# First layer's first channel product: 12 of 16 slabs as seven products of half sums, hidden chunks of 512

## The chip, the cores and the metric

The kernel runs on one core of a Trainium2 chip. The metric is the time of the program on the device, in microseconds (us), as the median of repeated runs. An engine executes its instructions in order: TensorE (PE: matmuls; its weight loads are listed as PEld), VectorE (DVE), ScalarE (ACT), GpSimd (POOL) and SyncE (SP, which issues nearly all transfers). Between engines, semaphores hold an instruction back until what it reads is written, or what it overwrites has been read.

## What is computed

Two layers over 768 tokens, 512 latent and 256 context, each of width 1024. A layer has a token-mixing sub-layer (convolution and attention) and a channel sub-layer, an MLP with squared ReLU. Shift, scale and gate of each sub-layer come from a modulation vector through `w_ada`.

```python
def sqrelu_mlp(h, w1, w2):
    return jnp.square(jax.nn.relu(h @ w1)) @ w2
...
        x = x + gx2 * sqrelu_mlp(modulate(rmsnorm(x, norm2_g[i]), sx2, ax2), w_mlp1[i], w_mlp2[i])
        if not last:
            h_ctx = h_ctx + gc2 * sqrelu_mlp(modulate(rmsnorm(h_ctx, norm2_g[i]), sc2, ac2),
                                             w_mlp1[i], w_mlp2[i])
```

`w_mlp1` is 1024 x 4096, `w_mlp2` 4096 x 1024. The change concerns `h @ w1` of the first layer, where all 768 tokens go through; in the last layer only the 512 latent tokens do.

## The kernel before

Each fp32 operand is split into a part of less precision and its residue, "hi" and "lo" (`split`, lines 76 and 77: the hi on ACT, the lo on DVE or POOL), and each product is three matmuls, hi x hi, hi x lo, lo x hi (`mm3`, lines 109 to 111). Tokens are the columns of a matmul; the features lie on the 128 partitions, in 8 pieces `k`.

The first layer's channel sub-layer begins when the norm `norm_mod` (line 341 scales on DVE, 345 shifts on ACT, 349 takes residues on DVE, others on POOL; `nsq`, `acc`, `nc`, `ms`, `dg`, `nb` are the squares, their sum and its root) writes `h2hh` and `h2hl`, the hi and lo of the modulated tokens, in three token groups: columns 0, 256 and 512 (the last is the context). The residual stream is `X`. Then four chunks of 1024 hidden features follow, loop `for cch in range(4)` from line 1436. In a chunk four slabs of 256 columns of `w_mlp1` are loaded (`r_w`, split into `h_w` and `l_w`), and `hidden` makes 128 hidden features of a token group as 8 x 3 matmuls into a PSUM bank `f`, then Relu, Square and Square on ACT (1443 to 1445, with the scratch `fr`) and the residue on DVE (1446): `fh` and `fl`. A group that starts at column 0 uses two banks of one pool, the groups that start at 256 or 512 two of another. In the first chunk the first two slabs go by three groups of 256 tokens, since the norm delivers so; all other slabs by 512 and 256. Then `out_slabs` multiplies the chunk's hidden values by 1024 rows of `w_mlp2` (banks `r`) and adds the gated result to `X` (line 1360).

Beside it runs the modulation product of the next layer, in steps between blocks (`ada_step`, `ada_rows`): 48 loads `ar` of 512 KB of `w_ada`, each multiplied by the two vectors and summed into `adaac` on DVE (line 282), then transposed and reduced (`adat`, `adp`). The next layer's small parameters are loaded ahead of it (`layer_params`: `sm`, `lp`, `cs`).

The source code gives order and priorities; a scheduler puts each engine's instructions into a row, and pools of a fixed number of buffers decide what can be issued when. Line 1420 opens the pool of the modulation's loads; the scratch tiles `fr` have three buffers of their own, the norm's scratch `nu` three others.

## Time and profile before

| | us |
|---|---|
| median of 3 runs (lowest, highest) | 2323.01 (2318.35, 2323.18) |
| the profiled execution | 2321.48 |
| its span | 2319.7 |
| first matmul of the first layer's hidden blocks | 820.94 |
| stage shown below | 820 to 1364 |

The profile is one execution. PE, DVE and so on are engines; an entry names line, engine, operation, and the tiles written and read, with partitions x elements and a count. A list of groups has the busy time and the mean length of one in ns, then the idle time of the engine ahead of them with what ended it. In a timeline a row has its start and its length. A row of stretches has the busy time of each engine, then the granted clock of PE, the share of the transfer engines that is busy, and GB/s.

### The profile page before, as it was taken

The numbers are of one execution on the slowest core, as the hardware profiler recorded it, in microseconds if no ns is written. First come the engines' busy times: TensorE is split into PE (matmuls) and PEld (weight loads), VectorE is DVE, ScalarE is ACT, GpSimd is POOL, SyncE is SP. The second block draws the span as 40 slices with busy tenths as digits, with TensorE's granted clock in tenths as the row PEclk, the third lists the DMA queues.
The fourth block names the chain that finished last, engine by engine and source line by source line (L and its number), as shares of the span: only waits on it lengthen the run. The fifth ranks groups of instructions, "written<-read, shape, count | busy, mean of one in ns | idle before, by whom it ended". The sixth has DMA issues, their size and how long they took to land.

```text
span 2319.7 us, 36413 instructions
## 1 busy us (share of the span) xinstructions
PE 2254.4 (97%) x14554; PEld 2022.3 (87%) x14554; DVE 1551.9 (67%) x2720; ACT 1027.0 (44%) x1997; POOL 684.4 (30%) x789
## 2 busy tenths in 40 slices
PE   8999999999999999999999998999999999999999
PEld 6999998888878998888888998999977879888887
DVE  6777776599657445555545567776759965757673
ACT  5555655522323263242524345565643333654542
POOL 1966764110000042323232347676611000100000
PEclk9999999999999999999999999999999999999999
DMA  9211111134534323433434422111113423442251
GB/s 309 63 37 41 46 47 45 44 132 141 161 128 155 106 66 118 128 108 124 131 102 135 110 65 58 44 37 49 44 62 123 134 86 115 155 127 91 73 182 37
DMA packets 217770, 229.48 MB, mean 99 GB/s; under 512 B 7472, under 2 KB 197376, under 8 KB 217472
## 3 DMA queue, kind: packets, MB, share of 16 engines
q1 hardware_dynamic: 217600, 227.15, 30.7%
q8 instruction: 114, 1.87, 0.3%
q14 instruction: 56, 0.46, 0.1%
HBM read 211.36 MB, written 15.77 MB: 98 GB/s over the span
## 4 chain that ended last, share of the span: by engine, by line
PE 81%; DVE 9%; POOL 4%; ACT 3%; DMA 2%; issue 1%; SPq 0%; DVEq 0%; POOLq 0%; ACTq 0%
PE f L109 6%; PE f L110 6%; PE f L111 6%; PE r L109 6%; PE r L111 6%; PE r L110 6%; PE gt L109 2%; PE qk L109 2%; PE gt L110 2%; PE gt L111 2%; PE qk L110 2%; PE qk L111 2%; DVE cacc L1163 2%; PE o L109 2%; PE o L110 2%; PE o L111 2%
## 5 line engine op out<-in xcount | busy, mean ns | idle before, releaser
L109 PE MATMUL f<-h2hh,h_w 128*128 128x512 f32 (+1 forms) x832 | 282.1, 342 | 1.7 <-ACT h2hh L76 1.5
L110 PE MATMUL f<-h2hl,h_w 128*128 128x512 f32 (+1 forms) x832 | 282.7, 341 | 1.0 <-POOL h2hl L77 1.0
L111 PE MATMUL f<-h2hh,l_w 128*128 128x512 f32 (+1 forms) x832 | 281.5, 340 | 0.0
L77 POOL TENSOR_TENSOR l_w<-r_w,h_w 128x1024 fp32r<-128x1024 f32 x64 | 158.5, 2498 | 334.9 <-ACT h_w L76 334.9
L1163 DVE SCALAR_TENSOR_TENSOR cacc<-z,cols,cacc 128x783 f32<-128x783 f32 (+1 forms) x240 | 207.7, 916 | 0.3
L109 PE MATMUL qk<-h_wqk,h1h 128*128 128x256 f32 x640 | 182.6, 288 | 2.1 <-ACT rw L755 1.3
L109 PE MATMUL r<-fh,h_w 128*128 128x256 f32 (+1 forms) x576 | 183.6, 319 | 0.0
L110 PE MATMUL r<-fl,h_w 128*128 128x256 f32 (+1 forms) x576 | 183.4, 319 | 0.0
L111 PE MATMUL r<-fh,l_w 128*128 128x256 f32 (+1 forms) x576 | 183.2, 318 | 0.0
L110 PE MATMUL qk<-l_wqk,h1h 128*128 128x256 f32 x640 | 180.2, 284 | 0.0
L111 PE MATMUL qk<-h_wqk,h1l 128*128 128x256 f32 x640 | 176.3, 284 | 0.3 <-POOL h1l L77 0.3
L110 PEld LDWEIGHTS f<-h2hl,h_w 128*128 128x128 f32 x832 | 157.5, 190 | 19.4 <-POOL h2hl L77 1.8
L109 PEld LDWEIGHTS f<-h2hh,h_w 128*128 128x128 f32 x832 | 156.6, 189 | 20.5 <-ACT h2hh L76 1.9
L927 DVE TENSOR_REDUCE st<-S 128x1 f32<-128x768 f32 (+1 forms) x160 | 134.4, 845 | 57.7 <-PE S L925 56.5
L111 PEld LDWEIGHTS f<-h2hh,l_w 128*128 128x128 f32 x832 | 157.3, 189 | 17.4
L282 DVE SCALAR_TENSOR_TENSOR adaac<-ar,cvec,adaac 128x256 f32<-128x256 f32 x336 | 144.2, 493 | 20.5 <-ACT adaac L279 15.2
L930 ACT ACTIVATE e<-S,st 128x768 f32<-128x768 f32 (+1 forms) x160 | 131.0, 821 | 40.1 <-DVE st L927 39.8
L76 ACT ACTIVATE h_w<-r_w 128x1024 fp32r<-128x1024 f32 x96 | 96.4, 1051 | 101.2 <-issue 44.5
L109 PE MATMUL gt<-h1h,h_wg 128*128 128x512 f32 (+1 forms) x384 | 138.2, 360 | 0.0
L110 PE MATMUL gt<-h1l,h_wg 128*128 128x512 f32 (+1 forms) x384 | 136.7, 356 | 0.0
L111 PE MATMUL gt<-h1h,l_wg 128*128 128x512 f32 (+1 forms) x384 | 136.5, 356 | 0.0
L109 PEld LDWEIGHTS qk<-h_wqk,h1h 128*128 128x128 f32 x640 | 122.1, 191 | 4.4 <-ACT rw L755 1.5
(307 smaller groups left out, 6636.3 us busy)
## 6 DMA issues: line engine op xcount, KB each, us to landing
r_w<-in_w_mlp_dram SPq DMA_DIRECT2D x64, 1024.0 KB, 5.3
ada<-in_w_ada_dram SPq DMA_DIRECT2D x24, 1024.0 KB, 5.6
ar<-in_w_ada_dram SPq DMA_DIRECT2D x48, 512.0 KB, 3.5
r_wqk<-in_w_in_dram SPq DMA_DIRECT2D x32, 512.0 KB, 5.1
r_wg<-in_w_in_dram SPq DMA_DIRECT2D x16, 1024.0 KB, 5.1
r_wv<-in_w_in_dram SPq DMA_DIRECT2D x8, 1024.0 KB, 5.2
r_wao<-in_w_attn_out_dram SPq DMA_DIRECT2D x8, 1024.0 KB, 5.2
r_wo<-in_w_out_dram SPq DMA_DIRECT2D x8, 1024.0 KB, 5.3
```

What stands on the lines that cost most here:

```text
L76: nc.scalar.activation(out=hi, in_=src, func=AF.Copy)
L77: return (lo_eng or nc.vector).tensor_tensor(out=lo, in0=src, in1=f32(hi), op=ALU.subtract)
L109: nc.tensor.matmul(ps, sh, mh, start=first, stop=False)
L110: nc.tensor.matmul(ps, sh, ml, start=False, stop=False)
L111: nc.tensor.matmul(ps, sl, mh, start=False, stop=last)
L282: nc.vector.scalar_tensor_tensor(out=a[:, q], in0=r[:, j], scalar=cvec[:, k, q : q + 1], in1=a[:, q], op0=ALU.mult, op1=ALU.add)
L927: nc.vector.tensor_reduce(out=st[:, m : m + 1], in_=S[:, :nkey], axis=AX.X, op=ALU.max, negate=True)
L930: nc.scalar.activation(out=e[:, :nkey], in_=S[:, :nkey], func=AF.Exp, bias=st[:, m : m + 1], accum_out=st[:, 2 + m : 3 + m])
L1163: nc.vector.scalar_tensor_tensor(out=ca[cc][:, :CV], in0=zt[cc][:, t : t + CV], scalar=wcol, in1=ca[cc][:, :CV], op0=ALU.mult, op1=ALU.add)
```

## The change

The hidden features go in eight chunks of 512 (two slabs of 256). Chunks 0 and 7 are made as before, by `hidden`. In chunks 1 to 6 each slab is seen as a 2 x 2 block product (features in halves of 512, hidden columns in halves of 128, tokens in halves of 384), and `seven` makes it from seven products instead of eight: sums and differences of weight quarters (`sums_f`, `sums_b`, on DVE) by sums and differences of token quarters (`token_sums`, on DVE, kept as hi and lo in `TS`, one in place of a quarter that is saved to DRAM and brought back before chunk 7). A product (`product`) is 4 pieces x 3 matmuls of 384 columns into one of the four banks of `mi_`; the sums of products go to `G` on DVE, Relu and squares on ACT to `F`, a single buffer for the hidden values. `second` multiplies each of chunks 0 to 5 by 512 rows of `w_mlp2`; the last two go together through `out_slabs`. The raw weights are in pieces of half a slab with three buffers.

The scratch of the small parameters, of the modulation sums and of the first chunk's `fr` now comes from the norm's three buffers (tag "u"). The modulation loads are 96 x 256 KB, with two buffers; the first eight slabs of 256 columns are multiplied by both vectors, the other sixteen, two at a time, by the latent one alone. Modulation steps start with the first hidden block.

```diff
+    def t2k(name):
+        if state["nt"]:
+            return state["tp"].tile([P, 512], F32, tag="t2k", bufs=state["nt"], name=name)
+        return state["xp"].tile([P, 512], F32, tag="u", bufs=3, name=name)
...
+        if state["nraw"] == 3:
+            rs = [state["tp"].tile([P, half, shape[1]], F32, tag="raw", name=f"r_{name}_{n}", bufs=3)
+                  for n in range(2)]
...
+        plan = [(s, 2 * k, 2) for s in range(8) for k in range(4)]
+        plan += [(s, k, 1) for s in range(8, 24, 2) for k in range(8)]
...
+            r = state["tp"].tile([P, 512], F32, tag="araw", bufs=2, name=f"ar{i}_{s}_{k}")
+            r = r.rearrange("p (k n) -> p k n", k=nq)
+            nc.sync.dma_start(r, rows(w_ada[i], 256 * s, 512 // nq)[:, k : k + nq])
...
+            state["tp"], state["nraw"], state["nt"] = gp, 3, 0
+            HT, HK = NT // 2, KT // 2
+            N0, N1, K0, K1 = slice(0, HT), slice(HT, NT), slice(0, HK), slice(HK, KT)
+            tt = nc.vector.tensor_tensor
+            F = gp.tile([P, 2, HK, NT], F32R, tag="F", name="F")
+            TS = gp.tile([P, 3, 2, HK, HT], F32R, tag="TS", name="TS")
+            TF = TS.rearrange("p a b k n -> p (a b k n)")
+            G = gp.tile([P, 4, HT], F32, tag="G", name="G")
+            GF = G.rearrange("p a n -> p (a n)")
+            F7 = TF[:, : 2 * HK * NT].rearrange("p (b k n) -> p b k n", b=2, k=HK)
+            b12_d = dpool.tile([2, P, HK, HT], F32, name="b12_d")
+            hl2 = h2h, h2l
+            B11, B12, B21, B22 = ([t[:, k, n] for t in hl2]
+                                  for k, n in ((K0, N0), (K0, N1), (K1, N0), (K1, N1)))
+            T1, T3, T4 = ([TS[:, a, j] for j in range(2)] for a in range(3))
+            T2 = B12
...
+            def squares(x, hi, lo):
+                nc.scalar.activation(out=hi, in_=x, func=AF.Square)
+                nc.scalar.activation(out=x, in_=x, func=AF.Square)
+                state["done"] = tt(out=lo, in0=x, in1=f32(hi), op=ALU.subtract).ins
...
+            def token_sums():
+                for j in range(2):
+                    nc.sync.dma_start(b12_d[j], f32(B12[j]))
...
+                g0, g1 = G[:, 0:2], G[:, 2:4]
+                for ks in (slice(0, 2), slice(2, 4)):
+                    b11, b12, b21, b22, t1, t3, t4 = (
+                        [x[:, ks] for x in b] for b in (B11, B12, B21, B22, T1, T3, T4))
+                    yield from sums(g0, f32(b12[0]), (less, b11[0]), (plus, b12[1]), (less, b11[1]))
+                    yield from sums(g1, f32(b22[0]), (less, b12[0]), (plus, b22[1]), (less, b12[1]))
+                    split(*t1, g0)
+                    yield
+                    yield from sums(g0, g1, (plus, b11[0]), (plus, b11[1]))
+                    split(*t3, g1)
+                    yield
+                    yield from sums(g1, g0, (less, b21[0]), (less, b21[1]))
+                    split(*b12, g0)
+                    yield
+                    split(*t4, g1)
+                    yield
+
+            raws, wts, sms = {}, {}, {}
...
+            def sums_f(c, s):
+                sm = sms[c, s] = gp.tile([P, HK, P], F32, tag="sm", name=f"sm{c}_{s}")
+                a11, a12, a21, a22 = quarters(c, s)
+                tt(out=a21, in0=a11, in1=a21, op=ALU.subtract)
+                tt(out=sm, in0=a22, in1=a21, op=ALU.subtract)
+
+            def fill_a(c, s):
+                sm = sms[c, s]
+                a11, a12, s3, _ = quarters(c, s)
+                w = wts["a", c, s] = pair_tiles((4, HK, P), f"a{c}_{s}")
+                for n, src in enumerate((a11, sm, a12, s3)):
+                    split(w[0][:, n], w[1][:, n], src, nc.gpsimd if n == 2 else None)
...
+            def product(w, n, b, name):
+                ps = mi_.tile([P, 512], F32, tag="mi", name=name)[:, :HT]
+                for k in range(HK):
+                    mm3(ps, (w[0][:, n, k], w[1][:, n, k]), (b[0][:, k], b[1][:, k]),
+                        k == 0, k == HK - 1)
+                return ps
...
+                w = wts.pop(("a", c, s))
+                nc.scalar.activation(out=s11, in_=product(w, 0, B11, nm + "1"), func=AF.Copy)
+                tt(out=s22, in0=s11, in1=product(w, 1, T2, nm + "6"), op=ALU.add)
+                fill_b(c, s)
+                if (c, s) == (6, 1):
+                    for j in range(2):
+                        for k in (slice(0, 2), slice(2, 4)):
+                            r = raw_half(f"b12_{j}_{k.start}", (2, HT))
+                            nc.sync.dma_start(r, b12_d[j][:, k])
+                            nc.scalar.activation(out=B12[j][:, k], in_=r, func=AF.Copy)
+                tt(out=s11, in0=s11, in1=product(w, 2, B21, nm + "2"), op=ALU.add)
+                done(0)
+                tt(out=s21, in0=s22, in1=product(w, 3, T3, nm + "7"), op=ALU.add)
+                ahead()
+                w = wts.pop(("b", c, s))
+                ps = product(w, 0, T1, nm + "5")
+                tt(out=s12, in0=s22, in1=ps, op=ALU.add)
+                tt(out=s22, in0=s21, in1=ps, op=ALU.add)
+                done(3)
+                tt(out=s12, in0=s12, in1=product(w, 1, B22, nm + "3"), op=ALU.add)
+                done(1)
+                later()
+                tt(out=s21, in0=s21, in1=product(w, 2, T4, nm + "4"), op=ALU.subtract)
+                done(2)
...
+            for g in halves:
+                for s in range(2):
+                    for m in range(2):
+                        hidden(0, s, m, g, F, xp.tile([P, 512], F32, tag="u", bufs=3,
+                                                      name=f"fr{s}_{m}_{g.start}"))
+                        ada_step()
+                        if (s, m) == (0, 1) and g is CTXS:
...
+            for c in range(7):
+                if c:
+                    seven(c, 0, lambda: next_f(c), lambda: sums_b(c, 1))
+                    seven(c, 1, lambda: next_r(c))
+                if c == 6:
+                    break
+                fill_r(c, 1, (nc.gpsimd, nc.gpsimd))
+                load_f(c + 1, 0)
+
+                def tick(m, g):
+                    if c == 0:
+                        sum_step(2)
+                    else:
+                        ada_step()
+
+                second(c, 0, tick)
+                load_f(c + 1, 1)
+                sums_f(c + 1, 0)
+                fill_a(c + 1, 0)
+                second(c, 1, tick)
+                sums_b(c + 1, 0)
+                drain(sums)
...
+                        o = 512 * ((4 * s + 2 * m + (g is not LAT)) % 3)
+                        hidden(7, s, m, g, F7, GF[:, o : o + 512])
+                        ada_step()
+                        if g is LAT:
+                            ada_step()
```

What the change does to the rows of three engines, at the start of the stage. Names: `nu_n2_0_512` is the norm's scratch for the context group, `f` and `fr` the hidden blocks and their scratch, `adaac` the modulation sums.

On ACT, where the first Relu of a hidden block stands (before: behind the scale of the second group's norm):

```order
L317 ACTIVATE dg_n2_0_256_9121<-cst_75,ms_n2_0_256_9118 128x128 [waits Pool_49]
L1443 ACTIVATE fr0_0_0_0_9424<-f0_0_0_0_9399 128x256 [waits PE_49]
L1444 ACTIVATE fh0_0_0_9383<-fr0_0_0_0_9424 128x256 [waits Activation_49]
L1445 ACTIVATE fr0_0_0_0_9424<-fr0_0_0_0_9424 128x256 [waits Activation_49]
L345 ACTIVATE h2hh0_8460<-nu_n2_0_256_0_9126,ad0_143 128x256 [waits DVE_49]
```

In the changed kernel the same Relu, now line 1481, comes after the last piece of the context group's norm:

```order
L365 ACTIVATE h2hh0_8463<-nu_n2_0_512_6_9335,ad0_143 128x256 [waits DVE_49]
L76 ACTIVATE TS_9350<-G_9351 128x768 [waits DVE_49,PE_49]
L365 ACTIVATE nu_n2_0_512_7_9339<-nu_n2_0_512_7_9339,ad0_143 128x256 [waits DVE_49]
L76 ACTIVATE h2hh0_8463<-nu_n2_0_512_7_9339 128x256 [waits Activation_49]
L1481 ACTIVATE fr0_0_0_9389<-f0_0_0_0_0_9390 128x256 [waits DMAHW0_49,PE_49,Pool_49]
L1473 ACTIVATE F_9349<-fr0_0_0_9389 128x256 [waits Activation_49]
```

It has moved past 29 rows: the norm of two groups, four squares and one split of a token sum. On PE before, the third block of the first group follows directly on the second:

```order
L110 MATMUL f0_0_1_0_9429<-h2hl0_8461,h_w1_0_0_0_9222 128x256
L111 MATMUL f0_0_1_0_9429<-h2hh0_8460,l_w1_0_0_0_9223 128x256
L109 MATMUL f0_0_2_0_9459<-h2hh0_8460,h_w1_0_0_1_9288 128x256 [waits Activation_49]
L110 MATMUL f0_0_2_0_9459<-h2hl0_8461,h_w1_0_0_1_9288 128x256
L111 MATMUL f0_0_2_0_9459<-h2hh0_8460,l_w1_0_0_1_9289 128x256
```

Now two blocks of the second group come in between, and then the third block (`f0_0_1_0_0`) stands behind the context group's norm and the small parameters:

```order
L125 MATMUL f0_0_0_1_256_9580<-h2hh0_8463,l_w1_0_0_0_9226 128x256
L354 MATMUL nc_n2_0_512_9297<-cst_75,acc0_2_8454 128x1 [waits DVE_49,PE_49]
L343 MATMUL nb_n2_0_512_9306<-dg_n2_0_512_9303,cst_75 128x256 [waits DVE_49]
L182 MATMUL smps1_9355<-cst_75,sm1_9353 128x128 [waits DMAHW0_49,PE_49]
L182 MATMUL smps1_9355<-cst_75,sm1_9353 128x128
L123 MATMUL f0_0_1_0_0_9467<-h2hh0_8463,h_w1_0_0_1_9291 128x256 [waits Activation_49]
```

Between the second and the third block of the first group stand the 48 matmuls of two blocks of the second group and these five small ones, and the third block waits for ACT. On DVE before, the residues of the first chunk's context group and the first modulation sums:

```order
L1446 TENSOR_TENSOR fl0_0_2_9388<-fr0_0_2_512_9724,fh0_0_2_9387 128x256 [waits Activation_49]
L1446 TENSOR_TENSOR fl0_0_3_9390<-fr0_0_3_512_9754,fh0_0_3_9389 128x256 [waits Activation_49]
L1446 TENSOR_TENSOR fl0_0_4_9392<-fr0_0_4_0_9792,fh0_0_4_9391 128x512 [waits Activation_49]
L282 SCALAR_TENSOR_TENSOR adaac1_0_9799<-ar1_0_9797,cvec_332,adaac1_0_9799 128x256 [waits DMAHW2_49]
L282 SCALAR_TENSOR_TENSOR adaac1_0_9799<-ar1_0_9797,cvec_332,adaac1_0_9799 128x256 [waits DVE_49] x4
```

In the changed kernel, ahead of the eighth block: the residues `F` of the second group, token sums into `G` and modulation sums in turn, and a split of `G` that ACT begins (line 76) and DVE ends (line 77).

```order
L1475 TENSOR_TENSOR F_9349<-fr1_1_0_9502,F_9349 128x256 [waits Activation_49]
L301 SCALAR_TENSOR_TENSOR adaac1_0_9423<-ar1_0_4_9428,cvec_332,adaac1_0_9423 128x256 [waits DVE_49]
L77 TENSOR_TENSOR TS_9350<-G_9351,TS_9350 128x768 [waits Activation_49]
L301 SCALAR_TENSOR_TENSOR adaac1_0_9423<-ar1_0_4_9428,cvec_332,adaac1_0_9423 128x256 [waits DVE_49] x2
L1475 TENSOR_TENSOR F_9349<-fr0_0_256_9538,F_9349 128x256 [waits Activation_49]
L1490 TENSOR_TENSOR G_9351<-h2hh0_8463 128x768 [waits DVE_49]
L301 SCALAR_TENSOR_TENSOR adaac1_0_9423<-ar1_0_6_9464,cvec_332,adaac1_0_9423 128x256 [waits DMAHW5_49,DVE_49]
L1490 TENSOR_TENSOR G_9351<-G_9351,h2hl0_8464 128x768 [waits DVE_49]
```

Token sums and modulation sums have moved in among the residues; before, the modulation began only after the residues of the context group.

More of the change, by code (lines that the diff above doesn't have):

```diff
@@ L1408, in mlp1_slab @@
         def mlp1_slab(cch, s):
-            w1[cch, s] = load_slab(rows(w_mlp1[i], 1024 * cch + 256 * s, 256),
+            w1[cch, s] = load_slab(rows(w_mlp1[i], (1024 if last else 512) * cch + 256 * s, 256),
                                    f"w1_{i}_{cch}_{s}", lo_eng=None if last else nc.gpsimd)
@@ L1491, in after @@
             def after(s):
-                if fin:
-                    nc.sync.dma_start(xs_d[i + 1][:, 2 * s : 2 * s + 2, :],
-                                      X[:, 2 * s : 2 * s + 2, :])
+                nc.sync.dma_start(xs_d[i + 1][:, 2 * s : 2 * s + 2, :],
+                                  X[:, 2 * s : 2 * s + 2, :])
             out_slabs(
                 lambda s: load_slab(
-                    w_mlp2[i][1024 * cch : 1024 * cch + 1024, 256 * s : 256 * s + 256]
-                    .rearrange("(k p) n -> p k n", p=P), f"w2_{i}_{cch}_{s}", lo_eng=nc.gpsimd),
-                lambda k: (fh[k], fl[k]), gate2, f"r{i}_{cch}",
-                norm1 if fin else None, after, tick=ada_step, ahead=
-                (lambda: first.update(w=qk_slab(i + 1, 0, nc.gpsimd)),
-                 v_first) if fin else ())
-        if not last:
-            rpool.__exit__(None, None, None)
+                    w_mlp2[i][3072:4096, 256 * s : 256 * s + 256]
+                    .rearrange("(k p) n -> p k n", p=P), f"w2_{i}_{s}", lo_eng=nc.gpsimd),
+                lambda k: tuple((F if k < HK else F7)[:, j, k % HK] for j in range(2)),
+                gate2, f"r{i}", norm1, after, ahead=
+                (lambda: first.update(w=qk_slab(i + 1, 0, nc.gpsimd)), v_first))
             state["ada_done"] = True
-            ada_gain(Ln, 1)
+            ada_gain(Ln, 1, ns=1)
             L = Ln
```

234 lines of the change are left out of this document (154 added, 80 removed).

## The prediction

> **What bounds the kernel now.** The busy table of the page comes first, then the chain that ended last, then the busy time by stretches of the first layer's channel sub-layer.
>
> ```profile
> PE 2254.4 (97%) x14554; PEld 2022.3 (87%) x14554; DVE 1551.9 (67%) x2720; ACT 1027.0 (44%) x1997; POOL 684.4 (30%) x789
> PE 81%; DVE 9%; POOL 4%; ACT 3%; DMA 2%; issue 1%; SPq 0%; DVEq 0%; POOLq 0%; ACTq 0%
> 820.00:1364.00 544.00, 542.97 (x3415) 491.80 (x3413) 285.87 (x598) 204.89 (x376) 170.70 (x80) 1.00 0.36 112
> 820.00:860.00 40.00, 38.97 (x311) 37.65 (x310) 20.11 (x47) 26.51 (x67) 18.44 (x15) 1.00 0.17 54
> 1985.00:2310.00 325.00, 325.00 (x1516) 272.32 (x1516) 208.04 (x273) 154.75 (x213) 2.98 (x4) 1.00 0.33 109
> ```
>
> PE carries 81% of the chain. The stage that is changed runs from 820 to 1364 us; in a row of stretches the columns are PE, PEld, DVE, ACT, POOL, clock, DMA share, GB/s. PE is busy for 542.97 of 544.00 us, at clock 1.00. DVE has 286 us of work there, ACT 205, POOL 171. So the stage is as long as its matmuls, and fewer columns through PE shorten it as long as nobody else becomes late. The last row is the last layer's channel sub-layer, which already uses seven products (of 512 columns): 325.00 of 325.00 us busy, so the scheme as such can be fed.
>
> **What is removed: PE time.** A matmul costs the distance between starts, not its length, since they overlap.
>
> ```profile
> 899.74 0.39 PE L109 MATMUL r<-fh,h_w 128*128 128x512 f32 x1
> 900.42 0.39 PE L109 MATMUL r<-fh,h_w 128*128 128x512 f32 x1
> ...
> 827.07 0.28 PE L111 MATMUL f<-h2hh,l_w 128*128 128x256 f32 x1
> 829.95 0.28 PE L111 MATMUL f<-h2hh,l_w 128*128 128x256 f32 x1
> ```
>
> Three of 512 columns take 0.68 us, 0.2267 each; 24 of 256 take 2.88 us, 0.120 each. For 384 columns the middle, 0.173 (estimate; its bounds are those two). A slab of 256 hidden columns cost 2 blocks x 8 k x 3 = 48 matmuls of each width: 48 x 0.3467 = 16.64 us. As seven products it costs 7 x 4 x 3 = 84 of 384: 14.56 us. Twelve slabs save 12 x 2.08 = **25.0 us**. The four plain slabs and the second product keep their matmuls and widths. With PE dense, the profiled execution's 2321.5 us would become 2296.5.
>
> **What is added: DVE time, most of it at the start.** New on DVE are twenty wide ops of token sums and their residues, the weight sums, the sums of products, and the modulation product of the next layer, which starts earlier. In the order of the changed kernel, DVE goes from the third norm op of the second column group (after 827 us) to the last residue but one of the first chunk's hidden values, through 56 two-operand ops of 256 (22 of the norm, 34 of the modulation), 15 differences of 256, 18 ops of 768, one of 1024, two transposes and two reductions of 512, and some 15 small ones. The prices:
>
> ```profile
> 826.39 1.27 DVE L341 SCALAR_TENSOR_TENSOR nu_n<-X,A,nb_n 128x256 f32<-128x256 f32 x3 [5.06 <-PE nb_n L323]
> 827.57 0.42 DVE L1446 TENSOR_TENSOR fl<-fr,fh 128x256 fp32r<-128x256 f32 x1
> ...
> 875.79 0.42 DVE L1446 TENSOR_TENSOR fl<-fr,fh 128x256 fp32r<-128x256 f32 x1
> 876.13 2.06 DVE L282 SCALAR_TENSOR_TENSOR adaac<-ar,cvec,adaac 128x256 f32<-128x256 f32 x5
> ...
> L77 DVE TENSOR_TENSOR l_w<-r_w,h_w 128x1024 fp32r<-128x1024 f32 x32 | 38.0, 1221 | 30.8 <-ACT h_w L76 30.7
> L77 DVE TENSOR_TENSOR h2hl<-fr,h2hh 128x512 fp32r<-128x512 f32 x16 | 11.0, 685 | 1.4 <-ACT h2hh L76 1.4
> L292 DVE STREAM_TRANSPOSE adat<-adaac 128x512 f32<-128x512 f32 x24 | 16.9, 703 | 0.0
> L293 DVE TENSOR_REDUCE adp<-adat 128x16 f32<-128x512 f32 x24 | 16.5, 688 | 0.8
> ```
>
> Three norm ops fill 826.39 to 827.57: 0.39 each. A difference of 256 fills 875.79 to 876.13: 0.34. An op of 768 isn't in this stage; its bounds are 0.685 and 1.221, the middle is 0.95, less 0.08 for overlap as in the rows above: 0.87. The sum: 56 x 0.39 + 15 x 0.34 + 18 x 0.87 + 1.14 + 2 x 1.35 + about 3 = **49 us**, against 34.6 us of PE (288 matmuls of 256) in the same place. In the kernel before DVE had 20.11 us in those first 40 us.
>
> That this delays PE follows from the orders. The scratch of the first hidden blocks is now one of the three buffers that the norm uses. So on ACT the first Relu stands behind the whole norm of the context group, and PE, whose banks for that group are full after four blocks, has nothing but the small matmuls of that norm in between. The norm's time in the kernel before:
>
> ```profile
> 835.08 0.98 DVE L361 TENSOR_TENSOR acc<-acc,nsq_so 128x256 f32<-128x256 f32 x2 [0.50 <-ACT nsq_so L360]
> 839.25 0.16 DVE L312 TENSOR_SCALAR ms_n<-nc_n 128x2 f32<-128x2 f32 x1 [2.84 <-PE nc_n L334]
> 839.55 0.70 POOL L313 TENSOR_TENSOR ms_n<-ms_n,mhalf 128x2 f32<-128x2 f32 x1 [4.29 <-DVE ms_n L312]
> 840.29 0.48 DVE L319 TENSOR_SCALAR dg_n<-cst,ms_n 128x128 f32<-128x128 f32 x2 [0.88 <-POOL ms_n L313]
> ```
>
> The last squares were summed at 836.1; the chain through POOL to the scale takes 840.8 - 839.2 = 1.6 us and two small matmuls, so the norm ops start between 836 and 838.5 (ACT has twelve ops less ahead, which may win two us). Four blocks end near 834: PE waits from there. DVE then does eight norm ops, four residues and five of the sums of 768 in order, 9 us, so the first Relu comes near 848. From there on each Relu stands behind a split of the token sums on ACT, which waits for DVE: the Relu that releases the eighth block stands behind the split that waits for the 16th wide op. Up to that op DVE has 26 x 0.39 + 16 x 0.87 + 5 x 0.34 + 3 = 28.8 us from 836 to 838.5, and perhaps 1.5 of waits for POOL's residues: 866 to 869. PE would have come to that block at 820.9 + 168 x 0.12 = 841. Five blocks are left, 14.4 us: the second product begins at about 882 to 885 instead of 820.9 + 34.6 = 855.5, that is 27 us late. The kernel before lost some 3 us here (1.03 us idle in its first 40, the rest in stretched matmuls). **Net 24 us**, bounds 16 (below, the lighter start) and 31 (the wide ops at 1.15, 18 x 0.28 more, and 2 us of holds).
>
> PE also comes back slowly from an idle stretch:
>
> ```profile
> 1742.52 0.60 PE L109 MATMUL cg<-h1h,h_wcg 128*128 128x512 f32 x1 [2.49 <-ACT sg L704]
> 1742.92 0.63 PE L110 MATMUL cg<-h1l,h_wcg 128*128 128x512 f32 x1
> 1743.34 0.63 PE L111 MATMUL cg<-h1h,l_wcg 128*128 128x512 f32 x1
> ...
> 1746.28 0.39 PE L109 MATMUL cg<-h1h,h_wcg 128*128 128x512 f32 x1
> 1746.50 0.40 PE L110 MATMUL cg<-h1l,h_wcg 128*128 128x512 f32 x1
> ```
>
> After 2.49 us idle the matmuls start 0.42 apart until 1746, then 0.22: eight times 0.2, 1.6 us lost. DVE sets when the waits above end, so only the last of them can cost this on top (ahead of the five blocks): it lies within the 27. [...]
>
> **Later chunks.** In the second product of chunk 1 and the products of chunk 2, DVE has 56 modulation ops (22 us), 16 residual adds, 22 ops of 384 on products, 20 of 512 on weights, one of 1024 and four transposes with reductions, by
>
> ```profile
> L1360 DVE SCALAR_TENSOR_TENSOR X<-r,ad,X 128x256 f32<-128x256 f32 x47 | 22.5, 480 | 21.2 <-PE r L111 20.9
> L1360 DVE SCALAR_TENSOR_TENSOR X<-r,ad,X 128x512 f32<-128x512 f32 x24 | 18.0, 751 | 68.4 <-PE r L111 68.4
> ```
>
> less 0.08 each (0.40 and 0.67; 384 between them, 0.47 as the ops do without the scalar): 22 + 8.6 + 10.3 + 12.2 + 1.1 + 5.4 = 60 us, while PE needs 33.3 + 29.1 = 62.4. A share of 96% leaves no room for holds:
>
> ```profile
> 854.76 4.97 POOL L77 TENSOR_TENSOR l_w<-r_w,h_w 128x1024 fp32r<-128x1024 f32 x2 [2.59 <-ACT h_w L76]
> 857.38 2.97 DVE L1446 TENSOR_TENSOR fl<-fr,fh 128x256 fp32r<-128x256 f32 x2
> ```
>
> Two differences that take 0.42 each alone took 2.97 us while POOL ran: about 2.2 lost. POOL has some 12 us of residues in those 62.4. I take **5 us** of delay, from 60 and some 7 of holds against 62.4 (0 if the residues fall beside ops that read products, 12 if all of POOL's time is lost to DVE). The other chunks have fewer modulation ops (DVE about 18 of 29 us in the products): **2 us** (0 to 8) for the refills of the single buffer of hidden values. The last chunk waits for two weight residues of POOL: **1 us** (0 to 3).
>
> The sum: 2321.5 - 25.0 + 24 + 5 + 2 + 1 = 2328.5. The profiled execution lies 1.5 us under the median of the three runs, inside their spread of 2318.4 to 2323.2; I write **2329**.
>
> **The rivals.**
> - *The start is lighter.* If the wide sums run at the 512-wide price (0.61, so 18 x 0.26 = 4.7 us less), the norm starts at 836 (1.5 less than the middle) and POOL's residues are in time (1.5 less), the start costs 24 - 8 = 16; with 2 us later the time is 2321.5 - 25 + 18 = 2314.5. For it speaks that ACT has twelve ops less ahead of that norm; against it, 49 us of DVE beside 34.6 of PE. The change is faster as soon as start and later chunks together cost less than 20.
> - *The whole gain stays*: 2297. The last layer's 325.00 of 325.00 speaks for it; there, though, DVE had 64% of the time, here 140% at the start.
> - *POOL holds DVE all along.* Every weight and token sum reads two tiles of SBUF, as the op that took 2.97 us did, and POOL has residues in each of six chunks. One hold more of 2.2 us for which PE has to wait in each of them is 6 x 2.2 = 13 us: 2342. Against it speaks that DVE has slack from the third chunk on. [...]
> - *The change doesn't save what it says*: if 384 columns cost what a weight load takes, 84 x 0.19 = 16 us for a slab save 8 us in place of 25: 2346. The 0.120 of 256 columns, with a load each, speaks against it.
>
> ```profile
> L109 PEld LDWEIGHTS f<-h2hh,h_w 128*128 128x128 f32 x832 | 156.6, 189 | 20.5 <-ACT h2hh L76 1.9
> ```
>
> **How the numbers follow.** Forecast 0.50 (own range 2320 to 2338), lighter start 0.25, POOL's holds 0.16, whole gain 0.06, no saving 0.03. 0.2% is 4.6 us, about what a measurement of this kernel can tell from no change: 2318.4 to 2327.7 counts as the same. Of the forecast's 0.50 about 0.19 lies there, of the lighter start's 0.25 about 0.06. So slower 0.31 + 0.16 + 0.03 = 0.50, same 0.25, faster 0.19 + 0.06 = 0.25. The range is 2304 to 2345: it leaves out the whole gain, the last rival and the tails of the others.
>
> **What would show it.** Right: PE idle for 10 us or more between 833 and 850 with ACT's Relu named behind it, again near 860, and the second product starting near 883; DVE without gaps from 838 to 882; a slab's products 14.6 us apart; a chunk of 62.4 us from the third on. Wrong: the second product starting before 870 (then the start was over-counted and the kernel is faster), DVE ops of 768 under 0.7 us, or chunks of 66 us and more, which would mean holds or late weights.

## The result and the profile after

| | before | after |
|---|---|---|
| median of 4 runs, us (lowest, highest) | 2320.81 (2318.35, 2323.18) | 2353.93 (2353.87, 2354.75) |
| the profiled execution, us | 2321.48 | 2353.90 |
| its span, us | 2319.7 | 2352.1 |
| first layer's channel sub-layer, first block to the first `qk` matmul, us | 820.9 to 1364.3: 543.4 | 819.4 to 1399.0: 579.6 |

The changed kernel takes 1.0148 times as long, with a 95% interval of 1.0135 to 1.0161: 33 us slower. The forecast was 2329.0, its range 2304 to 2345, so the sign was right and the time lies outside. Two of the six runs of one kernel below (the second shift) went at a granted clock of 0.748 and took 2745 us; its ratio and its times leave them out.

The busy table of the changed kernel's page and its chain that ended last:

```profile
PE 2247.9 (96%) x14402; PEld 2030.8 (86%) x14402; DVE 1688.1 (72%) x2808; ACT 1046.9 (45%) x2055; POOL 646.4 (27%) x783
PE 62%; DVE 19%; DMA 7%; ACT 5%; POOL 4%; issue 3%; SPq 0%; DVEq 0%; POOLq 0%; ACTq 0%
```

PE had 81% of the chain before and has 62% now. The next view cuts the stage at its phases: the first chunk's blocks, its second product, chunks 1 to 5 (products, then second product), the products of chunk 6, and the rest. The columns are the engines' busy times, the clock, the DMA share and GB/s, as before.

```profile
819.40:883.30 63.90, 44.81 (x303) 42.53 (x304) 52.69 (x110) 37.02 (x80) 17.17 (x13) 0.81 0.25 78
883.30:922.50 39.20, 36.66 (x202) 32.06 (x201) 32.12 (x45) 7.85 (x12) 6.59 (x3) 0.96 0.19 59
922.50:987.00 64.50, 62.67 (x360) 58.38 (x359) 52.23 (x93) 25.90 (x50) 13.22 (x7) 1.00 0.32 99
987.00:1055.40 68.40, 63.78 (x362) 58.62 (x361) 61.74 (x111) 26.18 (x49) 14.16 (x7) 0.98 0.40 127
1055.40:1123.10 67.70, 64.80 (x363) 60.24 (x362) 52.97 (x76) 24.33 (x46) 13.23 (x7) 0.97 0.42 130
1123.10:1192.70 69.60, 65.29 (x362) 59.96 (x360) 50.70 (x76) 24.73 (x46) 13.46 (x7) 0.98 0.40 124
1192.70:1261.70 69.00, 64.66 (x362) 59.91 (x361) 51.78 (x78) 24.71 (x46) 12.84 (x7) 0.98 0.40 123
1261.70:1293.40 31.70, 29.41 (x169) 28.80 (x167) 18.72 (x30) 17.27 (x33) 3.88 (x3) 1.00 0.46 138
1293.40:1399.00 105.60, 104.55 (x787) 100.18 (x787) 50.71 (x80) 42.56 (x80) 38.94 (x19) 1.00 0.30 98
```

Against dense matmuls (34.6, 33.3, 62.4 for a chunk, 29.1, by the prediction's prices) the start is 29.3 us longer, the second product of chunk 0 5.9, chunks 1 and 2 together 8.1, chunks 3 to 5 together 19.1, the products of chunk 6 2.6. DVE is busy for 51 to 52 us of 69 in chunks 4 and 5, so it has time to spare there, and still each of them is 7 us too long. What PE waits for in this stage, the longest groups of the table of waits (total, times, longest):

```profile
PE p L123 <- DVE G L1606: 10.3, 5, 2.5
PE smps L182 <- DMA sm<-in_small_dram: 10.0, 1, 10.0
PE r L135 <- DVE F L1475: 8.1, 5, 2.4
PE f L123 <- ACT fr L1481: 6.5, 3, 3.0
PE r L132 <- ACT F L1473: 3.9, 1, 3.9
```

The first and the third come five times: the waits of line 1606 fall into chunks 2 to 6 (0.7 us in chunk 2, 2.2 to 2.5 in the others), those of line 1475 end chunks 0, 1, 3, 4 and 5. The 3.9 us for `F` end the products of chunk 2. The second and the fourth belong to the start. First the start, in the timeline (start, length, engine, operation, in brackets the idle time ahead and what ended it):

```profile
846.24 0.66 PE L182 MATMUL smps<-cst,sm 128*128 128x128 f32 x2 [9.99 <-DMA sm<-in_small_dram]
846.99 0.38 ACT L1481 ACTIVATE fr<-f 128x256 f32<-128x256 f32 x1 [0.73 <-PE smps L182]
...
865.74 0.84 ACT L76 ACTIVATE TS<-G 128x768 fp32r<-128x768 f32 x1 [0.94 <-DVE G L1490]
866.49 0.36 ACT L1481 ACTIVATE fr<-f 128x256 f32<-128x256 f32 x1
...
883.31 0.28 PE L132 MATMUL r<-F,whir 128*128 128x256 f32 x1
```

The first Relu comes at 846.99, the one that releases the eighth block at 866.49, directly behind the split of a token sum, and the second product starts at 883.31. The 10 us in front carry the name of a transfer: the small parameters `sm` now take their place in the norm's three buffers, so their load waits for the norm too, and PE has five small matmuls ahead of the third block.

In the second product of chunk 0 DVE's row is full until 912, and POOL lengthens two of its operations:

```profile
884.58 5.07 POOL L77 TENSOR_TENSOR wlor<-rr,whir 128x1024 fp32r<-128x1024 f32 x2 [2.81 <-ACT whir L76]
884.77 2.63 DVE L301 SCALAR_TENSOR_TENSOR adaac<-ar,cvec,adaac 128x256 f32<-128x256 f32 x1
887.32 3.15 DVE L1490 TENSOR_TENSOR G<-h2hh 128x768 f32<-128x768 f32 x1
893.52 0.51 PE L135 MATMUL r<-F,whir 128*128 128x256 f32 x2 [2.38 <-DVE F L1475]
```

The same operations take 0.47 and 0.95 us elsewhere in this row, so 4.4 us are lost beside POOL, and PE waits 2.38 us for a residue of `F` that stands behind them. Here, with no slack on DVE, load and holds do cost.

The same view in chunk 5, where the waits of the later chunks are:

```profile
1198.45 1.28 DVE L77 TENSOR_TENSOR wlob<-rf,whib 128x512 fp32r<-128x512 f32 x2
1199.15 0.38 SPq L1521 DMA_DIRECT2D rf<-in_w_mlp_dram  x1
1203.35 0.69 DVE L1549 TENSOR_TENSOR sm<-rf,rf 128x512 f32<-128x512 f32 x1 [3.16 <-DMA rf<-in_w_mlp_dram]
1203.96 0.55 DVE L1599 TENSOR_TENSOR G<-G,p 128x384 f32<-128x384 f32 x1
...
1211.32 0.54 DVE L1606 TENSOR_TENSOR G<-G,p 128x384 f32<-128x384 f32 x1
1212.01 0.66 PE L123 MATMUL p<-h2hh,whia 128*128 128x384 f32 x1 [2.50 <-DVE G L1606]
...
1227.48 5.19 POOL L77 TENSOR_TENSOR wlor<-rr,whir 128x1024 fp32r<-128x1024 f32 x2 [2.42 <-ACT whir L76]
1228.75 1.70 DVE L1548 TENSOR_TENSOR rf<-rf 128x512 f32<-128x512 f32 x1 [1.91 <-issue]
1230.38 3.18 DVE L1475 TENSOR_TENSOR F<-G,F 128x384 fp32r<-128x384 f32 x2
1233.14 0.74 PE L135 MATMUL r<-F,whir 128*128 128x256 f32 x4 [1.84 <-DVE F L1475]
```

Line 1549 is a weight sum for the next slab (`sums_f`). It needs a raw piece whose load SP issued only at 1199.15, after DVE's residue `wlob` of 1198.45 had begun to free one of three raw buffers. DVE stands still 3.16 us at it, and behind it in DVE's row stand the sums `G`, whose products were done. So the sum of line 1606 is late, a bank of `mi_` comes free late, and PE waits 2.50 us at the second of the next slab's seven products. At the chunk's end the same thing happens again: line 1548, the first weight sum of the next chunk, stands ahead of the last two residues of `F`, and PE waits for the second of them. That pair also takes 3.18 us in place of some 1.0, while POOL's two residues run; those 2.1 us alone are as long as PE's wait, so at the chunk's end this trace doesn't tell the weight sum from the hold. The chunk's 6.6 us are these two places: 2.50 and 1.84 us of idling, and most of the rest is the slow matmuls behind the first of them (below).

### The profile page after: what moved, and what is told of

It reads as the page before. It is cut to its first block, busy times and chain, and to the rows that moved or that the text cites. A ratio compares the mean times of both kernels' runs of the same rounds, so it can differ in the third digit from the quotient of the medians.

```text
span 2352.1 us, 36553 instructions
## 1 busy us (share of the span) xinstructions
PE 2247.9 (96%) x14402; PEld 2030.8 (86%) x14402; DVE 1688.1 (72%) x2808; ACT 1046.9 (45%) x2055; POOL 646.4 (27%) x783
## 3 DMA queue, kind: packets, MB, share of 16 engines
q8 instruction: 113, 1.85, 0.3%
## 4 chain that ended last, share of the span: by engine, by line
PE 62%; DVE 19%; DMA 7%; ACT 5%; POOL 4%; issue 3%; SPq 0%; DVEq 0%; POOLq 0%; ACTq 0%
DMA ar<-in_w_ada_dram 3%; PE r L123 3%; PE r L124 3%; PE r L125 3%; DVE cacc L1183 3%; PE f L123 3%; PE f L124 3%; PE f L125 3%; DVE adaac L301 2%; PE qk L123 2%; PE qk L124 2%; PE qk L125 2%; PE gt L123 2%; PE gt L124 2%; PE gt L125 2%
## 5 line engine op out<-in xcount | busy, mean ns | idle before, releaser
L123 PE MATMUL f<-h2hh,h_w 128*128 128x512 f32 (+1 forms) x448 | 155.6, 353 | 7.7 <-ACT fr L1481 6.5
L124 PE MATMUL f<-h2hl,h_w 128*128 128x512 f32 (+1 forms) x448 | 156.5, 351 | 1.3 <-POOL h2hl L77 1.1
L125 PE MATMUL f<-h2hh,l_w 128*128 128x512 f32 (+1 forms) x448 | 155.2, 349 | 0.8 <-POOL l_w L77 0.8
L132 PE MATMUL r<-F,whir 128*128 128x512 f32 (+1 forms) x384 | 124.5, 342 | 4.1 <-ACT F L1473 3.9
L132 PE MATMUL r<-F,wlor 128*128 128x512 f32 (+1 forms) x384 | 124.2, 342 | 0.0
L124 PEld LDWEIGHTS qk<-l_wqk,h1h 128*128 128x128 f32 x640 | 122.9, 192 | 0.3 <-POOL l_wqk L77 0.3
L125 PEld LDWEIGHTS qk<-h_wqk,h1l 128*128 128x128 f32 x640 | 120.6, 192 | 0.5 <-POOL h1l L77 0.5
L123 PE MATMUL v<-h_wv,h1h 128*128 128x256 f32 x384 | 111.5, 290 | 6.6 <-ACT rwc L839 2.8
L125 PE MATMUL v<-h_wv,h1l 128*128 128x256 f32 x384 | 109.2, 284 | 0.0
L124 PE MATMUL v<-l_wv,h1h 128*128 128x256 f32 x384 | 108.7, 283 | 0.0
```

The source lines that it names most:

```text
L123: nc.tensor.matmul(ps, sh, mh, start=first, stop=False)
L124: nc.tensor.matmul(ps, sh, ml, start=False, stop=False)
L125: nc.tensor.matmul(ps, sl, mh, start=False, stop=last)
L132: nc.tensor.matmul(ps, w[j][:, k, m0 : m0 + P], a(k)[0][:, toks], start=k + j == 0, stop=False)
```

## The experiments

Three theories of the 33 us. **Order**: DVE's row stands still at weight sums whose raw piece isn't there, and at the start ACT's Relu stands behind the norm; either is cured by another place in the row or another buffer. **Load**: DVE has too much work, wherever it stands. **Holds**: POOL's residues lengthen DVE's. A time below is of a single run (no interval) unless several are named; the kernel before took 2317.42 to 2320.74 in the single runs beside them. Of kernels that were run more often here, one spread over 0.9 us, another over 8.7, so single differences of a few us are not read. Most of such a difference can lie ahead of the change: in the kernels below the same 5763 matmuls precede the stage, and its first block starts between 817.7 and 823.8 us. So the length of the stage (first block to first `qk` matmul, 543.3 us before, 579.6 in the changed kernel) is given beside a time, and what an edit is worth is read from it.

**The start alone.** Two edits: the first chunk's scratch in a tile of its own, and the token sums told to stand behind the last residue of `F`.

```diff
+            frs = gp.tile([P, HK, P], F32, tag="sm", name="frs").rearrange("p k n -> p (k n)")
...
-                        hidden(0, s, m, g, F, xp.tile([P, 512], F32, tag="u", bufs=3,
-                                                      name=f"fr{s}_{m}_{g.start}"))
+                        hidden(0, s, m, g, F, frs[:, 256 * m : 256 * m + 256])
```

> The first chunk's scratch no longer shares the norm's three buffers (two halves of the tile of the weight sums, idle in that chunk); nothing else. Theory A (the shared buffers cost the start: they put the first Relu behind the context norm): of some 33 us lost between 820 and 900 about 20 vanish, 2333 us. Theory B (DVE has 49 us of work in a place where PE has 35, whatever the buffers): the first Relu comes 15 us sooner, but the second product starts only 3 to 8 us sooner, 2346 to 2351.

```diff
             def sum_step(n):
-                for _ in range(n):
-                    next(sums, None)
+                with tc.issue_after(state["done"]):
+                    for _ in range(n):
+                        next(sums, None)
```

> The token sums wait for the first residual adds, so none of them stands in the first chunk; scratch shared as in the changed kernel. Theory B: 16 wide ops of 0.87 us leave the start, the second product starts 10 to 14 us sooner (near 870); some 5 us come back before the first products, which wait for the sums: 2342 to 2348. Theory A: the Relu stays behind the norm, the start changes by less than 4 us: 2350 or more.

With its own scratch the second product starts at 866.4 instead of 883.3, 17 us sooner, and the kernel takes 2352.73, 1.2 us less than the median of the changed one. Neither forecast came: the start gained far more than the second had it, the whole far less than the first. The stage itself takes 572.4 us, 7.2 less: in this run it began 3.8 us later, and some 2 us were lost behind it. The table of waits of this kernel, over the same stage:

```profile
PE r L132 <- ACT F L1473: 9.9, 3, 6.0
```

The wait for `sm` is gone, and PE waits 9.9 us for `F` instead, the longest 6.0, and (not shown) 4.0 for DVE's `X`: of what the start won, chunks 0 to 2 took back 11.5 us. With the token sums behind the residues the second product starts at 877.7, 5.6 us sooner where 10 to 14 were expected, and the time is 2357.57 (stage 582.4, 2.7 longer). So less than half of what the start wins is kept as long as DVE's row stays as it is.

**The two places in a chunk.** One edit moves the weight sums of the next slab (`ahead`) behind the last sum of the fifth product, the other the first sums and splits of the next chunk behind the last residue of `F`; a third moves only POOL's residues behind that residue.

```diff
-                ahead()
                 w = wts.pop(("b", c, s))
                 ps = product(w, 0, T1, nm + "5")
                 tt(out=s12, in0=s22, in1=ps, op=ALU.add)
-                tt(out=s22, in0=s21, in1=ps, op=ALU.add)
+                state["g"] = tt(out=s22, in0=s21, in1=ps, op=ALU.add).ins
                 done(3)
+                with tc.issue_after(state["g"]):
+                    ahead()
```

> The second slab's weight sums and splits come two sums of products later on DVE. Theory C (a weight half that lands late blocks DVE's queue, and PE waits for a bank that a sum of products behind it would free): the five waits of products for a sum of products (10.3 us, and slow matmuls behind them) vanish, 2339 to 2343. Rival D (DVE is simply full there, or held by POOL): the waits move to the next product, 2350 or more.

```diff
-                sums_f(c + 1, 0)
-                fill_a(c + 1, 0)
+                with tc.issue_after(state["done"]):
+                    sums_f(c + 1, 0)
+                    fill_a(c + 1, 0)
```

> The next chunk's first weight sums wait for a residual add of the second product, so on DVE they no longer stand ahead of the last two residues of the hidden values. Theory E (DVE's queue stood still there, waiting for a weight piece whose raw buffer was not free): the waits of the second product for those residues (8.1 us, and the slow matmuls behind them) go; the product's waits for a sum stay at 10: 2339 to 2346. Rival D (POOL's residues or DVE's load make them late): 2350 or more.

```diff
-                fill_r(c, 1, (nc.gpsimd, nc.gpsimd))
+                with tc.issue_after(state["done"]):
+                    fill_r(c, 1, (nc.gpsimd, nc.gpsimd))
```

> POOL's residues of the second weight slab of the second product wait for the last residue of the hidden values. Theory D2 (POOL's two ops of 2.5 us hold DVE's last residues, for which the second product waits): the five waits of the second product for DVE (8.1 us) fall under 3, with slow matmuls gone 2342 to 2348. Rival (the residues wait for ACT's squares or the products, not for POOL): waits stay at 7 to 8 us, 2352 to 2356.

The first edit gives 2349.56 (stage 573.5, 6.1 shorter), and line 1606 is gone from the waits; in its place PE waits for the residue of the first weights, 6.5 us in four times. So it gains less than was expected, and the wait has in part moved to the next product, as the rival had it. The second gives 2352.83 (stage 577.5, 2.2 shorter), the wait for `F` 4.6 us instead of 8.1: half of it went, not all. The third gives 2361.12, 7 us more than the changed kernel, of which 4.5 lie ahead of the stage (582.4, 2.8 longer). Its end of chunk 5, in the timeline:

```profile
1235.47 1.55 DVE L1548 TENSOR_TENSOR rf<-rf 128x512 f32<-128x512 f32 x1 [2.16 <-DMA rf<-in_w_mlp_dram]
1236.94 3.18 DVE L1475 TENSOR_TENSOR F<-G,F 128x384 fp32r<-128x384 f32 x2
1239.71 0.74 PE L135 MATMUL r<-F,whir 128*128 128x256 f32 x4 [1.83 <-DVE F L1475]
```

The pair of residues takes 3.18 us as before, and POOL's two run from 1234.05 to 1239.24, so POOL was not moved away from `F`, and this run can't acquit the holds by itself; it does name the transfer that line 1548 waits for. Both of the first two edits together:

> f_behind and g_first together: both places where a weight sum blocks DVE's queue are moved. Theory E: a chunk from the third on takes 62.4 to 64 us in place of 69; five chunks, 2320 to 2332. Rival D: chunks stay above 66 us, 2340 or more.

2346.50, 7.4 us less than the changed kernel (stage 571.3, 8.3 shorter), and its end of chunk 5:

```profile
1223.14 2.39 POOL L77 TENSOR_TENSOR wlor<-rr,whir 128x1024 fp32r<-128x1024 f32 x1 [0.28 <-ACT whir L76]
1223.51 2.90 DVE L1475 TENSOR_TENSOR F<-G,F 128x384 fp32r<-128x384 f32 x2 [3.71 <-ACT G L1474]
1223.94 0.50 PE L132 MATMUL r<-F,whir 128*128 128x512 f32 x1 [0.48 <-ACT F L1473]
```

Here POOL lengthens the pair just the same (2.90 us in place of some 1.0), and PE waits 0.48 us: with the weight sum out of the way the same hold costs PE at most that. Chunks 4 and 5 take 64.3 and 64.5 us instead of 69.6 and 69.0. That is the order theory at these two places, with POOL's residues where they were. The time is the rival's all the same (2340 or more), for chunk 3 stays at 67.8 us, with a wait of 2.0 us for a residue of the moved weights (`wloa`), and chunk 2 at 71.1.

**Both parts together.** The two edits of the order and the scratch of its own; then, in the last kernel, the weight sums behind the sum of the seventh product, one product sooner.

> both_late, and the first chunk's scratch apart from the norm's buffers. Theory A2 (the shared buffers cost some 15 us at the start, which the blocked queue ate later in own_fr): 10 to 16 us below both_late. Theory B (DVE's load in the first three chunks decides): the second product starts sooner, but the first products don't, 0 to 5 us below both_late.

```diff
-                tt(out=s21, in0=s22, in1=product(w, 3, T3, nm + "7"), op=ALU.add)
+                state["g"] = tt(out=s21, in0=s22, in1=product(w, 3, T3, nm + "7"), op=ALU.add).ins
...
-                state["g"] = tt(out=s22, in0=s21, in1=ps, op=ALU.add).ins
+                tt(out=s22, in0=s21, in1=ps, op=ALU.add)
```

> both_own with the second slab's weight sums one product sooner, behind the sum that takes the fourth product (its raw piece has landed by then). If the waits of products for those weights (7.2 us on DVE's part, 3.0 on ACT's) come from the lateness alone: 2326 to 2331. If from DVE's load: 2333 or more.

2335.03 and 2327.22, both as expected of order and buffers. By the stage (555.9 and 552.4 us) the scratch that alone was worth 7.2 us is worth 15.4 on top of the order, and the one product 3.5; in the times it is 1.2, 11.5 and 7.8. So the two causes hide each other in part: where DVE's row stalls in every chunk, part of an earlier start only waits there. In the last one chunk 4 takes 63.1 us, and most of what is left is in chunks 0 to 2. Its longest wait there:

```profile
1001.79 2.60 DVE L1475 TENSOR_TENSOR F<-G,F 128x384 fp32r<-128x384 f32 x1
1004.31 2.96 DVE L301 SCALAR_TENSOR_TENSOR adaac<-ar,cvec,adaac 128x256 f32<-128x256 f32 x2
...
1008.75 0.58 PE L132 MATMUL r<-F,whir 128*128 128x256 f32 x1 [6.12 <-ACT F L1473]
```

In this place DVE is without a gap, and each of the two rows is some 2.1 us over its price (0.5 and 0.87 elsewhere in this trace) beside POOL's two residues of 1001.60 to 1006.59. So here, where DVE has no slack, the holds count, as in chunk 0 of the changed kernel.

**The load.** To price the modulation, these two kernels leave out the multiply-and-adds of six of its eight pieces for each column slab (their loads stay), the first in the changed kernel, the second with the order and the scratch (2335.03).

```diff
-                    else:
+                    elif k == KT - 1:
                         nc.vector.scalar_tensor_tensor(
```

> The changed kernel without six of the eight pieces of the next layer's modulation sums (144 two-operand ops of 256 and 48 of 512, some 88 us of DVE in the stage; transfers and transposes stay). Theory B (DVE's load in the first chunks decides, beside the order): 12 us leave the start and some 10 each chunk 1 and 2; the start stays behind the norm: 2328 to 2338. Theory A (order and buffers alone): the same waits stand in the same places, 2345 or more.

> The same left out of both_own (scratch apart, both weight sums late; 2335.0 us). Theory B: what is left there of waits in chunks 0 to 3 (some 30 us) shrinks to 10 or less, 2308 to 2318. If it is order and late weights that are left: above 2326.

Without the work the changed kernel takes 2343.67, 10 us less (stage 567.4) and still 26 over the kernel before (2317.42), between the two forecasts; PE waits for the residues of `F` 13.0 us in six times. Where the load counts is told by the stretch from chunk 3 to the products of chunk 6, which takes 238.00 us in the changed kernel, with DVE busy for 174.16. In this one:

```profile
1045.28:1283.15 237.87, 223.96 (x1249) 207.99 (x1247) 139.65 (x215) 91.28 (x170) 42.31 (x24) 0.98 0.39 125
```

DVE has 34 us less to do there, and the stretch is as long. So the load explains none of what the later chunks lost; its 12 us lie ahead of them. With the order mended the same work is worth 25 us (21 in the stage, 534.8): 2310.23, below the kernel before. Chunks 1 and 2 of that kernel, in the view of stretches:

```profile
901.50:962.00 60.50, 59.95 (x344) 55.24 (x343) 44.88 (x71) 27.30 (x51) 13.22 (x7) 1.00 0.39 127
962.00:1025.60 63.60, 63.22 (x367) 58.27 (x367) 45.27 (x71) 26.40 (x48) 13.33 (x7) 1.00 0.40 128
```

PE is dense there, with DVE at 45 us of 62; chunks 3 to 5 take 63.5 to 64.0. It computes less than the others, so its time is no candidate; it shows that seven products can be fed. Where PE is fed, matmuls of 384 columns start 0.173 us apart, as was estimated: in chunk 5 of the changed kernel 43 starts lie between 1195.67 and 1202.95.

**Can the modulation be put elsewhere?** Five kernels move its steps in time, and one only its folding. The first, on 2335.03, alternates those with two vectors (two multiply-and-adds for each piece) with those with one; the second does so on 2327.22, with no step in chunk 0, more in chunk 7, and the folding of the sums (`fold`: small matmuls `adaps`) later. The third and fourth take all twelve steps out of chunk 0 and leave 8 and 12 of 16 in chunks 1 and 2, with more in chunks 3 to 5 (20, 24, 24):

```diff
                 def tick(m, g):
                     if c == 0:
                         sum_step(2)
-                    else:
+                        return
+                    if g is LAT:
+                        ada_step()
+                    if g is not LAT and (c > 2 or c == 2 and m % 2):
+                        ada_step()
+                    if g is LAT and (c > 3 or c == 3 and m % 2):
                         ada_step()
```

> both_own, and the modulation's steps of one and of two vectors alternate in place of all two-vector steps first: DVE loses some 8 us of work in chunk 0 and 10 in each of chunks 1 and 2, and gets it back in chunks 3 to 7. Theory B: 8 to 18 us below both_own, under the kernel before. Theory A2 (load is no issue once the buffers are apart): within 4 us of both_own.

> own_p7 with the modulation's two-vector and one-vector steps alternating, none of them in chunk 0, one more for each block of chunk 7, and its two foldings later. Theory B: DVE's share falls under 90% in each of chunks 0 to 3, 2306 to 2318, faster than the kernel before. If the mixed order has other waits: above 2326.

> The same shift on both_own (2335.0 us), whose second weight sums come one product later. Theory B: 2314 to 2325, above p7_shift by the waits for late weights (some 6 us). Rival: above 2330.

> own_p7 (2327.2 us) with the modulation's steps moved off the full chunks, none left out: chunk 0 none in place of 12, chunk 1 8, chunk 2 12, chunk 3 20, chunks 4 and 5 24 each, chunk 7 12. Theory B (what is left in own_p7, some 8 us at the start and 17 in chunks 1 and 2, is DVE's load): DVE has 16 us less in chunk 0, 13 less in chunk 1, 6 less in chunk 2: 2308 to 2318, faster than the kernel before. Rival (it is the order, as best1 suggests, where spread steps put waits elsewhere): above 2324.

The mixes took 2335.94 and 2334.96 (stages 561.5 and 559.7), no better than what they were built on: the gain that the load theory forecast did not come. The shift on 2335.03 took 2347.18 (four runs, 2346.15 to 2347.80; ratio to before 1.0118, interval 1.0103 to 1.0134), that on 2327.22 took 2343.17 to 2350.67 in four runs, with the ratio 1.0123 (1.0106 to 1.0140); both are slower than what they were built on, against the forecast. Chunks 1, 2 and 3 of the first of the two:

```profile
903.70:966.10 62.40, 61.83 (x354) 57.03 (x353) 48.50 (x83) 24.57 (x45) 12.78 (x7) 1.00 0.30 94
966.10:1029.00 62.90, 62.66 (x358) 57.88 (x357) 52.27 (x89) 25.63 (x48) 13.27 (x7) 1.00 0.32 101
1029.00:1111.60 82.60, 64.75 (x367) 59.37 (x365) 72.32 (x130) 29.37 (x56) 14.84 (x8) 0.91 0.38 120
```

Chunks 1 and 2, which took 65.5 and 72.0 us in the kernel that this one is built on, are dense, so their loss was the modulation's share of DVE. Chunk 3 takes 82.6 us. The waits of the whole stage in this kernel say why:

```profile
PE adaps L271 <- DVE adp L313: 13.7, 1, 13.7
PE p L125 <- DVE wloa L77: 12.8, 3, 5.2
```

The small matmuls of the folding kept their early place in PE's row and now wait for steps that come later, and the rest waits for DVE's residues of weights. The last two put both foldings behind the last step, one with the steps where they were, one with none in chunk 0, 8 in chunk 1, 12 in chunk 2 and 24 in the last.

```diff
-                if s in (7, 22):
+                if s == 22:
                     yield
-                    fold(0 if nq == 2 else 8, part, nq)
+                    fold(0, parts[:, :, :32], 2)
+                    fold(8, parts[:, :, 32:64], 1)
```

> own_p7 with both foldings behind the last step and nothing else. If foldings cost nothing where DVE is not late: within 2 us of own_p7, 2325 to 2329.

> own_p7 with the modulation's steps moved as far as chunk 7 (none in chunk 0, 8, 12, 16, 16, 16 in chunks 1 to 5, 24 in chunk 7) and both foldings behind the last step, so that PE's row has no folding in chunk 3 (in own_shift one waited there for 13.7 us). Theory B: chunks 0 to 2 as in own_shift (some 2 us lost between 880 and 1040), chunks 3 to 6 under 3 us each: 2308 to 2320. Rival (moved steps fill the products of chunks 3 to 5 and hold the weight sums there): above 2326.

2330.46 (five runs, 2326.65 to 2335.35; ratio 1.0042, interval 1.0028 to 1.0057) and 2331.18 (four runs, 2327.16 to 2334.13; 1.0046, 1.0029 to 1.0062). The second reaches chunk 7 at 1258.0, the first at 1269.4, and both reach the end of the stage within 1.2 us of each other (1375.2, 1374.0). The second's waits from 1255 on:

```profile
PE r L124 <- DVE TS L1477: 6.6, 1, 6.6
PE adaps L271 <- DVE adp L314: 3.1, 1, 3.1
```

What it saved in the early chunks it pays in the last one. The stages of the two take 552.1 and 552.0 us, as long as that of 2327.22 (552.4), so the folding costs nothing in the stage (the time is 1.5 us above what was expected), and the moved steps gain nothing, as the rival had it. No kernel that does all the work beat the kernel before; the best that was run several times is 0.4% over it.

## Why the prediction was wrong

*The saving of 25.0 us* held: matmuls of 384 columns start 0.173 us apart where PE is fed. With the order mended and the modulation cut, chunks take 60.5 to 64.0 us against 62.4 forecast, and that kernel is below the kernel before.

*The start, "net 24 us"*, was right in its mechanism and nearly in size. The first Relu was forecast near 848 and came at 846.99, the releasing one at 866 to 869 and came at 866.49, the second product at 882 to 885 and came at 883.31: 27.8 us late against 27. The 10 us of idling in front carry the name of `sm`, not of ACT's Relu as forecast. What it had not: the second product of chunk 0 took 39.2 us in place of 33.3, with a wait of 2.4 us for a residue of `F` behind DVE's full row. The text stopped its sum where that product begins.

*Chunks 1 and 2, 5 us* (0 to 12): 8.1. The reason that was given, DVE's share, is about half of it: with the modulation cut and the order as it was, these chunks take 129.3 us in place of 132.9, 4.5 over the price, and they are dense only when the order is mended too.

*"2 us (0 to 8) for the refills of the single buffer of hidden values"* is the step that failed. Chunks 3 to 5 and the products of chunk 6 lost 19.1 + 2.6 = 21.7 us. The step was priced by DVE's share of time in the products (18 of 29 us), as if DVE's row could use its slack. It couldn't: it stood still at weight sums whose raw pieces had no buffer yet, in front of sums that PE's banks and `F` waited for. The order was there to be read; this is DVE's row in chunk 5 as the program has it:

```
L1549 TENSOR_TENSOR sm5_1_12624<-rf5_1_1_12394,rf5_1_0_12393 128x512 [waits DMAHW3_49]
L1599 TENSOR_TENSOR G_9351<-G_9351,p5_0_2_12588 128x384 [waits DVE_49,PE_49]
```

The prediction quoted such rows for the start only, and counted buffers only for `F`, not the three raw ones. Its prices give 3 x 62.4 + 29.1 = 216.3 us from chunk 3 to the first block of chunk 7; the kernels took:

| | us | over the prices |
|---|---|---|
| the changed kernel | 238.0 | 21.7 |
| the changed kernel, modulation cut | 237.9 | 21.6 |
| the first chunk's scratch apart | 240.5 | 24.2 |
| both weight sums moved | 228.8 | 12.5 |
| both moved, scratch apart | 226.6 | 10.3 |
| the same, one product sooner | 223.4 | 7.1 |
| both moved, scratch apart, modulation cut | 221.6 | 5.3 |

POOL is busy for 42 to 44 us of this stretch in each of them. So the place of the two weight sums in DVE's row is worth 9 of the 21.7 us by itself and, with the scratch apart and the one product, 15; the load alone is worth nothing. What the last 5 to 7 us are was not told apart.

*POOL's holds, 2.2 us in each chunk, 2342*: near the result in time, but not what most of the later chunks' loss came from: a held pair stands in a kernel whose PE hardly waits for it (2.90 us beside a wait of 0.48). At the end of the changed kernel's chunks the hold adds to the weight sum, and no run took it away alone. Holds count in chunk 0 of the changed kernel and in chunk 2 of the mended one, where DVE has no slack. The prediction's sign that chunks of 66 us and more "would mean holds or late weights" was met, mostly by the weights.

*That the saved matmuls don't pay*, the last rival, fell with the dense chunks. *The lighter start* and *the whole gain* fell with the start.

The sum: 2328.5 was forecast for the profiled execution, 2353.9 came, 25.4 us more. By the windows 2 of them are the start's, 6 the second product of chunk 0, 3 chunks 1 and 2, 20 the later chunks, and 1 the last chunk's blocks (35.2 us in place of 33.3, where 1 was forecast): 32. Against that the stage began 1.5 us earlier, and 2.3 us came back behind it (the stage ends 34.7 us later, the execution 32.4); some 3 us were not traced. One part stays open: how far DVE's load and how far POOL's holds in chunks 0 to 2 make up the 9 us by which the mended kernel's stage is longer than before (552.4 against 543.3) was not told apart, since no run took POOL's residues out of those chunks alone.

## What to carry to other kernels

Read an in-order row for what stands behind an instruction that waits for a transfer: count the buffers of what it reads, and put it behind whatever another engine is waiting for, even where the engine is idle a quarter of the time. Mend stalls that hide each other together before judging one of them (7 us of the stage alone, 15 on top of the other). Compare the length of the changed stage as well as the whole time: here what lies ahead of it moved by up to 6 us between runs of the same instructions. When work is moved to a quieter stretch, move its consumers in the other engines' rows too.

## What the runs showed of the hardware

A wait can cost more than its idle time. In chunk 5 PE idles 2.50 us, and the timeline of the changed kernel goes on like this:

```profile
1212.79 0.52 PE L125 MATMUL p<-h2hh,wloa 128*128 128x384 f32 x1
...
1214.70 0.49 PE L125 MATMUL p<-h2hh,wloa 128*128 128x384 f32 x1
1215.03 0.35 PE L123 MATMUL p<-h2hh,whia 128*128 128x384 f32 x1
1215.21 0.34 PE L124 MATMUL p<-h2hl,whia 128*128 128x384 f32 x1
```

Starts lie 0.32 us apart until 1215.03 and 0.175 after it: nine matmuls from 1212.01 take 3.0 us in place of 1.6. Behind the 1.84 us of idling at 1233.14 four matmuls of 256 columns take 0.58 us to the next start, 0.145 each against 0.12, and there is no such stretch. In the changed kernel's stage none follows the idle times of 1.6 to 2.2 us ahead of products and second products (the 2.20 at 1280.55 is the longest), and one follows those of 2.4 to 2.5. The length of the idle time alone doesn't tell: in the kernel before, 1.85 us of idling at 1858.44 are followed by such a stretch (matmuls of 512 columns 0.43 us apart from 1859.15 to 1862.13, 0.23 from 1862.43 on), while the 2.20 us at 1280.55 are not. What else decides it was not looked into.
